# Memory keys and values in float32 inside the experts' ring, expert rows fetched by plain loads and added on VectorE, one more ring tile

## The chip, the cores and the metric

The kernel runs on one core of one Trainium2 chip. The metric is the time of one execution on the device, in microseconds (us); of several runs the median is given.

## What is computed

Two transformer blocks, one after the other, on 512 tokens of width 1024. The first ends in a mixture of 32 experts of which each token uses two; the second mixes sparse attention, a convolution and attention over a memory of 256 rows. Cut to what the change touches:

```python
def hierarchical_moe(h, ...):          # end of the first block
    ...                                # two experts for each token, weights sum to the group's gate
    hid = silu(t @ w1[e]) * (t @ w3[e])
    y = sum over e of combine[:, e] * (hid @ w2[e])
x = x + hierarchical_moe(h2, ...)

def hybrid_layer(x, mem, norm_mix, w_in, ..., norm_mem, w_mem_kv, ...):   # the second block
    xn = rms_norm(x, norm_mix)
    proj = xn @ w_in                   # split into q, kv, gates, conv, q_mem, merge
    ...
    kvm = rms_norm(mem, norm_mem) @ w_mem_kv      # 256 x 1024 by 1024 x 1024
    km, vm = split(kvm)
    ...
```

## The kernel before

**Dense products.** A planner (`Dense`) holds a list of items in program order: weight tiles with their matmuls, and calls. `load` issues the transfer of every item whose ring has room, `prepare` makes the items ready, `step` issues one group of matmuls and, where an item has a `free`, gives its room back. Transfers are issued on SP's queue, in order: a transfer that waits for its tile holds all those behind it. Ordinary weight tiles of 1 MB go through ring "w" (`wraw`, two buffers) and are split into a high and a low part (`whi` by ScalarE at L290, `wlo` by VectorE at L291, two buffers each); a product is then three matmuls, high by high, low by high, high by low (L300 to L302).

**Experts.** 16 pairs of experts (L953 to L978), six tiles of 1 MB to a pair, 96 in all. Their float32 tiles are not split. They go through ring "m", which has no buffers of its own: `room_for` (L243) takes the first place with room among eight `mraw` ("p"), three more ("q"), one `uraw` ("u") and the buffers `wraw`, `whi`, `wlo` ("w", "h", "l", two each), 18 tiles together; `grant` (L178) gives and takes rooms. A pair has its tokens gathered, four tiles of up-projection (L891), then two of down-projection (L907); ScalarE copies the result out (`yt`, L912) and POOL scatters it into the DRAM tensor `y_d` (L913), where each token has two rows.

**Memory.** Midway through the experts, with four rooms taken from "p", `lay_mem` loads the memory, and `lay_mem2` normalises, transposes and splits it into two tiles (`memT`, high and low). After the experts come four column blocks of `w_mem_kv` (L980 to L995): each tile split, 48 matmuls, and a copy to `kvraw` by ScalarE. Blocks 0 and 1 are loaded by SP in ring "m"; blocks 2 and 3 are loaded by POOL's queue, each tied behind another instruction there (`load_behind`, L224).

**From one block to the next.** At L1217 every engine passes a branch for the case in which an expert has more tokens than its 64 places; in these runs it is not taken. Then eight accumulating transfers on POOL's queue add the rows of `y_d` to `x1` (printed as `x` in the trace; L1289 to L1296), four token tiles by two choices. Two column blocks of the second block's `w_in` (columns 2328 and 2584, the memory's queries) are loaded behind them. Per half (two token tiles) ScalarE sums squares (L1310), VectorE makes the reciprocal root and scales (`ny`, L1313), TensorE transposes, ScalarE and VectorE split into `xnT` (L235, L236), and then the `w_in` products begin. `x1` is also stored to DRAM by POOL (L1813).

Of the kernel before, what the change touches and what calls it, by code (L numbers as in the profile page):

```python
# [6 lines left out]
F32 = mybir.dt.float32  # L7
# [5 lines left out]
OP = mybir.AluOpType  # L13
# [8 lines left out]
CAP = 64  # L22
RING = 8
RING2 = 3
NE = 32
US = 1000.0

# [132 lines left out]
def _body(ctx, tc, I, out):  # L160
# [12 lines left out]
    dn = Dense()  # L173
    dn.room["w"] = 2
    dn.room["m"] = 0
    MR = {"room": {"p": 0, "q": 0, "u": 0, "w": 0, "h": 0, "l": 0}}

    def grant(n, at="p"):  # L178

# [38 lines left out]
    def behind(i, j):  # L218

        tc.add_manual_dep(i.ins, j.ins.name,  # L220
                          mybir.DependencyInfo(mybir.DependencyClass.NoSync, mybir.DependencyReason.DATA),
                          reason="order")

    def load_behind(ring, j):  # L224

        MODE["behind"] = j
        dn.room[ring] = 1
        dn.load()
        dn.room[ring] = 0
        MODE.pop("behind")  # L230

    def split_to(hi, lo, src, scale=None):

        if scale is None:
# [7 lines left out]

    def room_for(shape):  # L243

        at = next((a for a in "pquwhl" if MR["room"][a] > 0), "p")
        MR["room"][at] -= 1
        if at in "whl":
            tag = {"w": "wraw", "h": "whi", "l": "wlo"}[at]
            r = wp.tile(shape, F32, name=tag, tag=tag, bufs=2)
        elif at == "u":  # L250
            r = r0.tile(shape, F32, name="uraw", tag="U")
        else:
            r = MR[at].tile(shape, F32, name="mraw", tag="mraw")
        MR[id(r)] = at
        return r
# [12 lines left out]
    def wtile(parts, shape, pieces=None, pool_=(), ring="w"):  # L268

        shape = list(shape)  # L270

        def load():
            r = wp.tile(shape, F32, name="wraw", tag="wraw", bufs=2) if ring == "w" else room_for(shape)
            for dst, src in parts:
                if "behind" in MODE:
                    behind(pool.dma_start(dst(r), src), MODE["behind"])
                else:
                    sync.dma_start(dst(r), src)
            return r

        def split(r):
            if ring == "m":
                MR["room"][MR.pop(id(r))] += 1
            h = wp.tile(shape, F32R, name="whi", tag="whi", bufs=2)
            l = wp.tile(shape, F32R, name="wlo", tag="wlo", bufs=2)
            np_, by_pool = (pieces, pool_) if pieces else MODE["split"]
            n = shape[1] // np_
            for i in range(np_):
                sl = slice(i * n, i * n + n)
                act.activation(h[:, sl], r[:, sl], AF.Copy)  # L290
                (pool if i in by_pool else dve).tensor_tensor(l[:, sl], r[:, sl], raw(h[:, sl]), op=OP.subtract)  # L291
            return h, l
        return load, split
# [603 lines left out]
    def push_down(e):  # L897
        p, m = divmod(e, 2)
        own = slice(64 * m, 64 * m + 64)

        def g(wt):

            hs = HS[p]
            py = psd()
            for k in range(2):
                for q in range(2):
                    pe.matmul(py[64 * q:64 * q + 64], hs[:, k, own], wt[:, k, 512 * q:512 * q + 512],  # L907
                              start=k == 0, stop=k == 1)

            def late():  # L910
                yt = R["ep"].tile([128, 512], F32, name="yt", tag="yt", bufs=4)
                act.activation(yt, py, AF.Copy)  # L912
                st = pool.indirect_dma_start(  # L913
                    out=y_d.rearrange("r (q d) -> (r q) d", q=2),
                    out_offset=bass.IndirectOffsetOnAxis(ap=R["dest2"][:, e:e + 1].bitcast(U32), axis=0),
                    in_=yt, in_offset=None, bounds_check=4 * S - 1, oob_is_err=False)
                for o in ysc:
                    tc.declare_no_dep(st.ins, o, reason="each row belongs to one token and choice")
                ysc.append(st.ins)
                if e == NE - 3:  # L920
                    load_behind("z", st)
            dn.defer(late)
            return 4 * 4 * 216.0
        load, same, free = down_tile(e)
        dn.push(load, same, [g], ring="m", free=free)
# [10 lines left out]

    def lay_mem2():
        raws, gy = memT["x"]
        hl = [MR["p"].tile([128, 8, 256], F32R, name=f"memT{i}", tag="mraw") for i in range(2)]
        for t in range(2):  # L940
            ss, rr = small("nss", [128, 1], 4), small("nrr", [128, 1], 4)
            act.activation(gy[:, 1], raws[:, t], AF.Square, accum_out=ss)
            rsqrt(rr, ss, [128, 1], 1.0 / D, EPS)
            dve.scalar_tensor_tensor(raws[:, t], raws[:, t], rr, gy[:, 0], op0=OP.mult, op1=OP.mult)
            ts_ = slice(t * 128, t * 128 + 128)
            for hf in range(2):
                ps = transpose4(lambda k: raws[:, t, (4 * hf + k) * 128:(4 * hf + k) * 128 + 128])
                ks = slice(4 * hf, 4 * hf + 4)
                split_to(hl[0][:, ks, ts_], hl[1][:, ks, ts_], ps.rearrange("p (k s) -> p k s", k=4))
        memT["T"] = hl  # L950
        grant(2)

    for p in range(NP):  # L953
        push_up(p, 0)
# [9 lines left out]
        else:  # L964
            dn.call(lambda p=p: (dn.flush(), lay_h(p)))
        if p == NP // 2 - 2:
            dn.call(lambda: grant(-4))
        if p == NP // 2:
            dn.call(lay_mem)
        if p == NP - 4:  # L970
            dn.call(lambda: (grant(-2, "h"), grant(-2, "l")))
        if p == NP - 3:
            dn.call(lambda: grant(-1, "u"))
        if p == NP // 2 + 2:
            dn.call(lay_mem2)
    dn.call(lambda: turn_h(NP - 1))
    push_down(NE - 2)
    push_down(NE - 1)  # L978

    dn.call(dn.flush, "experts")  # L980
    for c in range(4):
        def g(wt, c=c):
            if c == 0:
                R["kv"] = r0.tile([128, 2, 2, 512], F32, name="kvraw", tag="U")
            ps = psd()
            for t in range(2):
                ts_ = slice(t * 128, t * 128 + 128)
                for k in range(8):
                    mm3(ps[:, 256 * t:256 * t + 256], memT["T"][0][:, k, ts_], memT["T"][1][:, k, ts_],
                        wt[0][:, k], wt[1][:, k], k == 0, k == 7)  # L990
            a, h = divmod(c, 2)
            dn.defer(lambda: act.activation(R["kv"][:, a, :, h * 256:h * 256 + 256],
                                            ps.rearrange("p (t w) -> p t w", t=2), AF.Copy))
            return 48 * 109.0
        dn.push(*wcols(w_mem, c * 256, 256, ring="m"), [g], ring="m" if c < 2 else "z", name="mem" if c == 3 else None)  # L995

    dn.until("up_b")
    m2s.close()
# [63 lines left out]
    grant(RING - 6)  # L1062
    dn.until("wo3")
    mts.close()
    xes, q2s, es = ExitStack(), ExitStack(), ExitStack()
    xep = sub(xes, "rows", side="right")
    R["xe"] = [xep.tile([128, D], F32, name=f"xe{i}") for i in range(2)]
    MR["q"] = sub(q2s, "moeraw2", RING2, "right")
# [8 lines left out]
    with ordered(nc.vector.engine, nc.scalar.engine, nc.tensor.engine):  # L1077
# [110 lines left out]
            last = dve.tensor_reduce(cw[own], t5[own, :, m], axis=AX.X, op=OP.add)  # L1188
        rts.close()
        R["ep"] = sub(es, "experts", 1, "right")  # L1190
        lay_x(0)

    with tc.issue_after(last.ins):
# [15 lines left out]
    dn.until("experts")  # L1209
    dn.ahead = 1  # L1210
    es.close()
    q2s.close()
    xes.close()

# [2 lines left out]
    with tc.If(nr > 0):  # L1217
        with tc.tile_pool(name="rest", bufs=1, side="right") as fp:
# [57 lines left out]
                        in_=yt, in_offset=None, bounds_check=2 * S - 1, oob_is_err=False)  # L1276


    w_in2 = I["w_in_2"][0]
    w_mo, w_no, w_co, w_o2 = (I[n][0] for n in ("w_mem_out_2", "w_nsa_out_2", "w_conv_out_2", "w_out_2"))  # L1280
    w_g2, w_u2, w_d2 = (I[n][0] for n in ("w_gate_2", "w_up_2", "w_down_2"))
    cw1, cw2 = I["cmp_w1_2"][0], I["cmp_w2_2"][0]
    x2_d = tc.dram_tile([128, 4, D], F32, name="x2_d")
    macc2_d = tc.dram_tile([128, 8, S], F32, name="macc2_d")
    yv = y_d.rearrange("(k t p) d -> p t k d", k=2, p=128)
    dense_N(w_in2, 2328, 256, lambda: xnT, lambda c, q, ps: ev_qm(c, q, ps),
            between=lambda: (lay_xn(2), lay_xn(3)))
    added = []
    for k in range(2):  # L1289
        for t in range(4):  # L1290
            added.append(pool.dma_start(x1[:, t], yv[:, t, k], accum_op=OP.add))
            if (k, t) == (0, 0):
                load_behind("z", added[-1])
            if (k, t) == (1, 1):
                load_behind("w", added[-1])
                dn.room["w"] = -1  # L1296
    brs = ExitStack()
    br_p = sub(brs, "branch", side="right")

# [7 lines left out]
    for q in range(2):  # L1307
        ss, rr = small("nss", [128, 2], 4), small("nrr", [128, 2], 4)
        for t in range(2):
            act.activation(ny[q][:, t], x1[:, 2 * q + t], AF.Square, accum_out=ss[:, t:t + 1])  # L1310
        rsqrt(rr, ss, [128, 2], 1.0 / D, EPS)
        for t in range(2):
            dve.scalar_tensor_tensor(ny[q][:, t], x1[:, 2 * q + t], rr[:, t:t + 1], R["g2"], op0=OP.mult, op1=OP.mult)  # L1313
# [493 lines left out]

    dn.call(lay_kv_mem)
    dense_N(w_in2, 2584, 256, X, lambda c, q, ps: ev_qm(1, q, ps))
    load_behind("w", added[-1])  # L1810
    dn.room["w"] = 1
    for t in range(4):
        behind(pool.dma_start(x2_d[:, t], x1[:, t]), added[-1])  # L1813
    lay_xn(0)
    lay_xn(1)
    dn.call(lambda: lay_qm(0))
# [226 lines left out]
```

## Time and profile before

| | us |
|---|---|
| median of three runs | 1792.62 (1791.51 to 1793.68) |
| the profiled execution | 1795.56 |
| its span in the trace | 1793.5 |
| TensorE busy (PE) | 1692.7, 94% of the span |
| VectorE, ScalarE, GpSimd busy | 947.6, 662.1, 285.7 |
| experts, first matmul to the last weight tile | 603.75 to 832.62 |
| last weight tile of the experts to the second block's first `w_in` block running without a break | 832.62 to 882.90 |

The busy shares are means over stages with different limits. In the experts' stage the transfer engines (DMA) are busy almost without a break; behind 883 us TensorE is; the 50 us between the two are a chain of small transfers, splits and norms.

### The profile page before, as it was taken

Reading aid. Unit: us, or ns where it says so; the run is one execution under the profiler, and the core shown is the slowest. Engines: PE = TensorE matmul, PEld = TensorE weight load, DVE = VectorE, ACT = ScalarE, POOL = GpSimd, SP = SyncE. Lnnn points to the kernel's source line nnn. Section 1 sums busy time; section 2 is a strip of 40 time slices with the busy share of each in tenths; the row PEclk is TensorE's granted clock in tenths of the full one; section 3 lists DMA queues with packets and bytes.
Section 4 is the critical chain, followed back from the end, with each engine's and each line's share of the span. In section 5 each row is a group of like instructions: output and inputs, shape, how many; then the busy total and the mean of one; then the engine's idle time right before and its main releaser. Section 6 shows DMA issues by size and latency. Waiting matters only on the chain.

```text
span 1793.5 us, 24558 instructions
## 1 busy us (share of the span) xinstructions
PE 1692.7 (94%) x9766; PEld 1373.6 (77%) x9766; DVE 947.6 (53%) x2001; ACT 662.1 (37%) x1128; POOL 285.7 (16%) x276
## 2 busy tenths in 40 slices
PE   7999999999999699887799988799999999999999
PEld 7888888889789455444789876588788988888887
DVE  7642367777753411111578789964467444444221
ACT  4222244454523122122435577566523322222111
POOL 1000000000012222112200178611001111111000
PEclk9999999999999799899899999899999999999999
DMA  6223322122348899998724311121243222222240
GB/s 205 94 71 117 118 84 82 48 83 83 141 141 314 324 411 415 418 416 298 218 94 118 118 48 47 71 94 48 88 142 122 83 94 94 94 94 94 83 141 35
DMA packets 151018, 263.87 MB, mean 147 GB/s; under 512 B 11771, under 2 KB 109766, under 8 KB 146550
## 3 DMA queue, kind: packets, MB, share of 16 engines
q1 hardware_dynamic: 131542, 220.03, 34.2%
q0 software_dynamic: 12400, 33.71, 6.1%
q10 hardware_dynamic: 6960, 8.56, 1.3%
q8 instruction: 77, 1.26, 0.3%
q14 instruction: 39, 0.32, 0.1%
HBM read 248.62 MB, written 18.87 MB: 149 GB/s over the span
## 4 chain that ended last, share of the span: by engine, by line
PE 41%; DVE 7%; ACT 2%; DMA 2%; issue 1%; POOL 0%; ACTq 0%; DVEq 0%; POOLq 0%
PE pd L300 11%; PE pd L301 11%; PE pd L302 11%; DVE oa L1756 3%; PE pa L301 2%; PE pa L300 2%; PE pa L302 2%; DMA x<-y_d 2%; DVE wlo L291 1%; PE pa L381 1%; PE pa L1646 1%; ACT whi L290 1%; DVE sn L1661 0%; DVE sden L1668 0%; DVE pt L236 0%
## 5 line engine op out<-in xcount | busy, mean ns | idle before, releaser
L291 DVE TENSOR_TENSOR wlo<-wraw,whi 128x2048 fp32r<-128x2048 f32 (+1 forms) x112 | 248.8, 2221 | 192.8 <-ACT whi L290 192.1
L290 ACT ACTIVATE whi<-wraw 128x2048 fp32r<-128x2048 f32 (+1 forms) x123 | 213.1, 1735 | 345.8 <-PE pd L301 198.8
L301 PE MATMUL pd<-wlo,hT 128*128 128x256 f32 x512 | 145.5, 284 | 1.5 <-DVE wlo L291 1.5
L300 PE MATMUL pd<-whi,hT 128*128 128x256 f32 x512 | 146.0, 285 | 0.0
L302 PE MATMUL pd<-whi,hT 128*128 128x256 f32 x512 | 145.2, 284 | 0.0
L302 PE MATMUL pd<-hnT,wlo 128*128 128x512 f32 x352 | 139.4, 396 | 0.0
L300 PE MATMUL pd<-hnT,whi 128*128 128x512 f32 x352 | 139.3, 396 | 0.0
L301 PE MATMUL pd<-hnT,whi 128*128 128x512 f32 x352 | 139.2, 395 | 0.0
L300 PE MATMUL pd<-xnT,whi 128*128 128x512 f32 (+1 forms) x280 | 114.3, 408 | 0.0
L301 PE MATMUL pd<-xnT,whi 128*128 128x512 f32 (+1 forms) x280 | 113.0, 404 | 0.0
L302 PE MATMUL pd<-xnT,wlo 128*128 128x512 f32 (+1 forms) x280 | 112.9, 403 | 0.0
L1750 POOL TENSOR_TENSOR oa<-oa,ctm 128x512 f32<-128x512 f32 x60 | 91.3, 1522 | 60.5 <-ACT ctm L1749 57.0
L301 PEld LDWEIGHTS pd<-wlo,hT 128*128 128x128 f32 x512 | 97.2, 190 | 2.6 <-DVE wlo L291 1.8
L300 PEld LDWEIGHTS pd<-whi,hT 128*128 128x128 f32 x512 | 97.4, 190 | 1.2 <-issue 0.9
L302 PEld LDWEIGHTS pd<-whi,hT 128*128 128x128 f32 x512 | 97.1, 190 | 0.9 <-issue 0.4
L870 DVE SCALAR_TENSOR_TENSOR sg<-sg,pd 128x256 f32<-128x256 f32 x16 | 6.7, 421 | 165.6 <-ACT sg L869 165.6
L891 PE MATMUL pd<-mraw,xs 128*64 128x256 f32 x624 | 77.6, 401 | 11.8 <-DMA mraw<-in_w 11.6
L300 PEld LDWEIGHTS pd<-hnT,whi 128*128 128x128 f32 x352 | 66.1, 188 | 16.0
L301 PEld LDWEIGHTS pd<-hnT,whi 128*128 128x128 f32 x352 | 66.1, 188 | 15.9
L302 PEld LDWEIGHTS pd<-hnT,wlo 128*128 128x128 f32 x352 | 66.1, 188 | 15.8
L300 PE MATMUL pd<-hT,whi 128*128 128x512 f32 x192 | 77.8, 405 | 0.0
L302 PE MATMUL pd<-hT,wlo 128*128 128x512 f32 x192 | 77.7, 405 | 0.0
(546 smaller groups left out, 4059.1 us busy)
## 6 DMA issues: line engine op xcount, KB each, us to landing
mraw<-in_w SPq DMA_DIRECT2D x59, 1024.0 KB
wraw<-in_w_in SPq DMA_DIRECT2D x41, 1024.0 KB
wraw<-in_w_gate SPq DMA_DIRECT2D x19, 1024.0 KB
wraw<-in_w SPq DMA_DIRECT2D x11, 1024.0 KB
wraw<-in_w_up SPq DMA_DIRECT2D x11, 1024.0 KB
wlo<-in_w SPq DMA_DIRECT2D x10, 1024.0 KB
whi<-in_w SPq DMA_DIRECT2D x10, 1024.0 KB
wraw<-in_w_down SPq DMA_DIRECT2D x10, 1024.0 KB
```

The lines of the kernel that those rows point to most:

```text
L290: act.activation(h[:, sl], r[:, sl], AF.Copy)
L291: (pool if i in by_pool else dve).tensor_tensor(l[:, sl], r[:, sl], raw(h[:, sl]), op=OP.subtract)
L300: pe.matmul(ps, ah, bh, start=start, stop=False)
L301: pe.matmul(ps, ah, bl, start=False, stop=False)
L302: pe.matmul(ps, al, bh, start=False, stop=stop)
L381: pe.transpose(ps[:, t * 128:t * 128 + 128], src_of(t), ident)
L870: dve.scalar_tensor_tensor(sg, sg, 1.0, hid[:, 0:256], op0=OP.add, op1=OP.mult)
L891: pe.matmul(ph[64 * m:64 * m + 64, 256 * j:256 * j + 256], XS[p][:, kt, 64 * m:64 * m + 64], wt[:, m, k], start=kt == 0, stop=kt == 7)
L1646: pe.matmul(ps[:, :nm], Q[:, 4 * g + i, qs], KS[:, br, g, x, :nm], start=x == 0, stop=x == 1)
L1750: pool.tensor_add(acc, acc, tm)
L1756: taps.append(lambda i=i: dve.scalar_tensor_tensor(acc, up[:, j, i:i + S], convw[:, i, j:j + 1], acc, op0=OP.mult, op1=OP.add))
```

## The change

The memory is kept as one float32 tile: no split, and each column block takes 16 float32 matmuls in place of 48. The tiles of `w_mem_kv` become items of the experts' ring as the experts' own are (`whole`): block 0 stands between two pairs of experts, blocks 1 to 3 directly behind the last expert. The rows of `y_d` are fetched by four plain loads of 1 MB on SP's queue into tiles `yk` of the ring, and eight additions on VectorE put them on `x1`; the accumulating transfers and `load_behind` go. A new place "s" holds one more ring tile, in memory that the router leaves free; "u" is taken away five pairs earlier and the two "w" rooms two pairs before the end; three rooms instead of four are taken for the memory. The `w_in` block 2328 becomes an item ahead of the point at which the planner stands when the experts end.

```diff
@@ room_for
-        at = next((a for a in "pquwhl" if MR["room"][a] > 0), "p")
+        at = next((a for a in "pqsuwhl" if MR["room"][a] > 0), "p")
@@ lay_mem2
-        hl = [MR["p"].tile([128, 8, 256], F32R, name=f"memT{i}", tag="mraw") for i in range(2)]
+        mT_ = MR["p"].tile([128, 8, 256], F32, name="memT", tag="mraw")
...
-                split_to(hl[0][:, ks, ts_], hl[1][:, ks, ts_], ps.rearrange("p (k s) -> p k s", k=4))
-        memT["T"] = hl
+                act.activation(mT_[:, ks, ts_], ps.rearrange("p (k s) -> p k s", k=4), AF.Copy)
+        memT["T"] = mT_
         grant(2)
+
+    def push_mem(c):
+        def g(wt):
+            if c == 0:
+                R["kv"] = r0.tile([128, 2, 2, 512], F32, name="kvraw", tag="U")
+            ps = psd()
+            for t in range(2):
+                ts_ = slice(t * 128, t * 128 + 128)
+                for k in range(8):
+                    pe.matmul(ps[:, 256 * t:256 * t + 256], memT["T"][:, k, ts_], wt[:, k], start=k == 0, stop=k == 7)
+            a, h = divmod(c, 2)
+            dn.defer(lambda: act.activation(R["kv"][:, a, :, h * 256:h * 256 + 256],
+                                            ps.rearrange("p (t w) -> p t w", t=2), AF.Copy))
+            return 64 * 109.0
+        v = w_mem.rearrange("(k p) c -> p k c", p=128)
+        load, same, free = whole(v[:, :, c * 256:c * 256 + 256], (128, 8, 256))
+        dn.push(load, same, [g], ring="m", free=free, name="mem" if c == 3 else None)
@@ experts' loop
-            dn.call(lambda: grant(-4))
+            dn.call(lambda: grant(-3))
         if p == NP // 2:
-            dn.call(lay_mem)
+            dn.call(lambda: (lay_mem(), grant(-1, "u")))
         if p == NP - 4:
             dn.call(lambda: (grant(-2, "h"), grant(-2, "l")))
         if p == NP - 3:
-            dn.call(lambda: grant(-1, "u"))
+            push_mem(0)
+        if p == NP - 2:
+            dn.call(lambda: grant(-2, "w"))
...
     push_down(NE - 2)
+    dn.call(lambda: dn.room.update(w=2))
     push_down(NE - 1)
 
     dn.call(dn.flush, "experts")
...
+    for c in range(1, 4):
+        push_mem(c)
+    w_in2 = I["w_in_2"][0]
+    dense_N(w_in2, 2328, 256, lambda: xnT, lambda c, q, ps: ev_qm(c, q, ps),
+            between=lambda: (lay_xn(2), lay_xn(3)))
@@ router's end
         rts.close()
         R["ep"] = sub(es, "experts", 1, "right")
+        MR["s"] = sub(q3s, "moeraw3", RING3)
+        grant(RING3, "s")
+        dn.load()
         lay_x(0)
@@ behind the branch
-    for k in range(2):
-        for t in range(4):
-            added.append(pool.dma_start(x1[:, t], yv[:, t, k], accum_op=OP.add))
...
+    yk = {}
+    for t in range(4):
+        yk[t] = MR["p"].tile([128, 2, D], F32, name="yk", tag="mraw")
+        sync.dma_start(yk[t], yv[:, t])
...
         for t in range(2):
+            for k in range(2):
+                dve.tensor_add(x1[:, 2 * q + t], x1[:, 2 * q + t], yk[2 * q + t][:, k])
             act.activation(ny[q][:, t], x1[:, 2 * q + t], AF.Square, accum_out=ss[:, t:t + 1])
```

The planner and the scheduler turn this into an order of instructions. On SP before, the second round of the experts' ring, 18 tiles, has its two `wraw` side by side (`in_w` are the experts' weights):

```order
L261 DMA mraw<-in_w 128x2x1024
L261 DMA uraw<-in_w 128x2x1024
L261 DMA wraw<-in_w 128x2x1024 x2
L261 DMA whi<-in_w 128x2048 x2
L261 DMA wlo<-in_w 128x2x1024 x2
```

After, on SP in the same round, the two turns of `wraw` are apart:

```order
L254 DMA uraw<-in_w 128x2x1024
L254 DMA wraw<-in_w 128x2048
L254 DMA whi<-in_w 128x2x1024 x2
L254 DMA wraw<-in_w 128x2048
L254 DMA wlo<-in_w 128x2x1024 x2
```

They are apart because a `w_in` tile (`in_w_in`, block 2328) has one of the two buffers; after, it stands on SP between the first expert tiles of the ring, while the products of `w_out` run:

```order
L268 DMA wraw<-in_w_up_b 128x8x256
L268 DMA wraw<-in_w_out 128x8x256 x4
L254 DMA mraw<-in_w 128x2x1024 x4
L268 DMA wraw<-in_w_in 128x8x256
L254 DMA mraw<-in_w 128x2x1024 x4
```

It keeps the buffer until it is split, towards the end of the experts, so that the ring has one `wraw` left of the two that were granted, and the second load of each round waits until TensorE is through with the first: 18 tiles in effect, as before.

On SP before, the end of the experts is two blocks of the memory and the branch:

```order
L261 DMA mraw<-in_w 128x2048 x2
L261 DMA wraw<-in_w 128x2048
L261 DMA mraw<-in_w 128x2048
L278 DMA mraw<-in_w_mem_kv 128x8x256 x2
L1217 COMPARE_AND_BRANCH
```

After, on SP, blocks 1 to 3 of the memory stand there, then two `w_in` tiles ahead of the branch:

```order
L254 DMA mraw<-in_w 128x2048 x4
L254 DMA mraw<-in_w_mem_kv 128x8x256 x2
L254 DMA wraw<-in_w_mem_kv 128x8x256
L1218 TENSOR_LOAD rounds
L1218 ISA x2
L268 DMA wraw<-in_w_in 128x8x256 x2
L1219 COMPARE_AND_BRANCH
```

and on SP behind the branch come the four loads of the expert rows:

```order
L1235 COMPARE_AND_BRANCH
L1235 UNCONDITIONAL_BRANCH
L1219 UNCONDITIONAL_BRANCH
L1290 DMA yk<-y_d 128x2x1024 x4
L268 DMA wraw<-in_w_in 128x8x24
```

Each of the two `w_in` loads ahead of the branch waits until VectorE has split the tile before it (2328, then 2584); the four `yk` loads now stand behind that.

On VectorE before, behind the branch, there are the splits of the memory's last blocks and the first half's norm:

```order
L1217 UNCONDITIONAL_BRANCH
L291 TENSOR_TENSOR wlo<-mraw,whi 128x2048 x3
L353 TENSOR_SCALAR rs_v<-nss 128x2
L354 TENSOR_SCALAR rs_i<-rs_v 128x2
L355 TENSOR_SCALAR nrr<-rs_i 128x2
```

After, the additions stand there, all eight of them ahead of the first half's `ny`:

```order
L1219 UNCONDITIONAL_BRANCH
L1305 TENSOR_TENSOR x_4749<-x_4749,yk 128x1024 x5
L343 TENSOR_SCALAR rs_v<-nss 128x2
L1305 TENSOR_TENSOR x_4749<-x_4749,yk 128x1024
L344 TENSOR_SCALAR rs_i<-rs_v 128x2
L345 TENSOR_SCALAR nrr<-rs_i 128x2
L348 TENSOR_TENSOR rs_a<-nrr 128x2
L349 SCALAR_TENSOR_TENSOR rs_a<-rs_a,rs_v 128x2
L350 SCALAR_TENSOR_TENSOR nrr<-rs_a,nrr 128x2
L1305 TENSOR_TENSOR x_4749<-x_4749,yk 128x1024
L351 TENSOR_TENSOR rs_a<-nrr 128x2
```

The additions of the second half have moved ahead of the first half's scaling.

## Rows read from the trace of the kernel before

**Rows 1.** The page: span, and busy time of each engine.

```profile
span 1793.5 us, 24558 instructions
PE 1692.7 (94%) x9766; PEld 1373.6 (77%) x9766; DVE 947.6 (53%) x2001; ACT 662.1 (37%) x1128; POOL 285.7 (16%) x276
```

**Rows 2.** Windows: stretch, length, busy of five engines, PE clock, DMA share, GB/s.

```profile
604.00:608.00 4.00, 4.00 (x28) 2.33 (x28) 1.05 (x5) 0.00 (x0) 0.99 (x1) 0.70 0.20 55
608.00:612.00 4.00, 4.00 (x40) 2.43 (x36) 0.00 (x0) 0.00 (x0) 0.00 (x0) 1.00 0.94 314
607.00:832.60 225.60, 202.21 (x1424) 109.19 (x1421) 31.65 (x73) 43.82 (x86) 44.03 (x43) 0.97 1.01 408
...
848.00:868.00 20.00, 17.54 (x148) 17.13 (x147) 4.59 (x2) 6.08 (x6) 8.43 (x11) 1.00 1.03 231
...
900.00:1000.00 100.00, 99.46 (x776) 93.14 (x775) 83.32 (x191) 48.84 (x91) 2.36 (x5) 1.00 0.41 125
```

**Rows 3.** Timeline of the experts, PE and SP's queue: start, length, engine, line, idle before.

```profile
603.75 8.41 PE L891 MATMUL pd<-mraw,xs 128*64 128x256 f32 x64
...
607.03 17.50 SPq L261 DMA_DIRECT2D mraw<-in_w  x9
...
700.41 1.95 PE L891 MATMUL pd<-mraw,xs 128*64 128x256 f32 x16
...
720.21 3.68 PE L891 MATMUL pd<-mraw,xs 128*64 128x256 f32 x16 [3.39 <-DMA mraw<-in_w]
725.45 3.68 PE L891 MATMUL pd<-mraw,xs 128*64 128x256 f32 x16 [1.56 <-DMA mraw<-in_w]
...
733.95 1.95 PE L891 MATMUL pd<-mraw,xs 128*64 128x256 f32 x16
```

**Rows 4.** Timeline from the last expert tile on, all engines.

```profile
832.62 1.94 PE L907 MATMUL pd<-mraw,hs 128*64 128x512 f32 x8 [0.64 <-DMA mraw<-in_w]
...
836.25 1.91 ACT L290 ACTIVATE whi<-mraw 128x2048 fp32r<-128x2048 f32 x1 [1.01 <-DMA mraw<-in_w_mem_kv]
838.20 2.29 DVE L291 TENSOR_TENSOR wlo<-mraw,whi 128x2048 fp32r<-128x2048 f32 x1 [12.22 <-ACT whi L290]
...
838.22 0.38 PE L300 MATMUL pd<-whi,memT 128*128 128x256 f32 x1 [3.66 <-ACT whi L290]
...
841.69 1.91 ACT L290 ACTIVATE whi<-mraw 128x2048 fp32r<-128x2048 f32 x1 [3.52 <-DMA mraw<-in_w_mem_kv]
...
844.98 0.41 PE L300 MATMUL pd<-whi,memT 128*128 128x256 f32 x1
...
845.23 0.99 POOL L1291 DMA_DIRECT2D x<-y_d  x1 [8.69 <-DMA y_d<-yt,dest]
...
845.50 0.28 PE L300 MATMUL pd<-whi,memT 128*128 128x256 f32 x1
...
845.62 0.28 PE L301 MATMUL pd<-wlo,memT 128*128 128x256 f32 x1
```

**Rows 5.** The chain of waits, in order of time: start, length, what.

```profile
848.03 15.29 DMA x<-y_d
...
863.84 12.74 DMA x<-y_d
...
882.90 0.58 PE pd L302
```

**Rows 6.** Timeline ahead of the first `w_in` product, all engines.

```profile
876.60 1.06 ACT L1310 ACTIVATE ny<-x 128x1024 f32<-128x1024 f32 x1 [1.39 <-DMA x<-y_d]
...
877.66 0.58 ACT L992 ACTIVATE kvraw<-pd 128x512 f32<-128x512 f32 x1
...
879.77 2.48 DVE L1313 SCALAR_TENSOR_TENSOR ny<-x,nrr,gain 128x1024 f32<-128x1024 f32 x2
```

**Rows 7.** Timeline of PE, a float32 product of the first block (L705).

```profile
260.59 0.39 PE L705 MATMUL pa<-vb,aT 128*128 128x128 f32 x2
...
263.40 0.61 PE L705 MATMUL pa<-vb,aT 128*128 128x128 f32 x4
```

More of the change, by code (lines that the diff above doesn't have):

```diff
@@ L24 @@
 RING2 = 3
+RING3 = 1
 NE = 32
@@ L175, in _body @@
     dn.room["m"] = 0
-    MR = {"room": {"p": 0, "q": 0, "u": 0, "w": 0, "h": 0, "l": 0}}
+    MR = {"room": {"p": 0, "q": 0, "s": 0, "u": 0, "w": 0, "h": 0, "l": 0}}
     def grant(n, at="p"):
@@ L222, in behind @@
                           reason="order")
[L224 to L230, printed above, removed]
     def split_to(hi, lo, src, scale=None):
@@ L274, in load @@
             for dst, src in parts:
[L275 to L278, printed above, removed]
+                sync.dma_start(dst(r), src)
             return r
@@ L919, in late @@
                 ysc.append(st.ins)
-                if e == NE - 3:
-                    load_behind("z", st)
             dn.defer(late)
@@ L977, in _body @@
     push_down(NE - 2)
+    dn.call(lambda: dn.room.update(w=2))
     push_down(NE - 1)
     dn.call(dn.flush, "experts")
[L981 to L995, printed above, removed]
+    for c in range(1, 4):
[3 more added lines that the diff above has]
+            between=lambda: (lay_xn(2), lay_xn(3)))
     dn.until("up_b")
@@ L1064, in _body @@
     mts.close()
-    xes, q2s, es = ExitStack(), ExitStack(), ExitStack()
+    xes, q2s, es, q3s = ExitStack(), ExitStack(), ExitStack(), ExitStack()
     xep = sub(xes, "rows", side="right")
@@ L1211, in _body @@
     es.close()
+    q3s.close()
     q2s.close()
@@ L1276, in _body @@
                         in_=yt, in_offset=None, bounds_check=2 * S - 1, oob_is_err=False)
-    w_in2 = I["w_in_2"][0]
     w_mo, w_no, w_co, w_o2 = (I[n][0] for n in ("w_mem_out_2", "w_nsa_out_2", "w_conv_out_2", "w_out_2"))
@@ L1285, in _body @@
     yv = y_d.rearrange("(k t p) d -> p t k d", k=2, p=128)
-    dense_N(w_in2, 2328, 256, lambda: xnT, lambda c, q, ps: ev_qm(c, q, ps),
-            between=lambda: (lay_xn(2), lay_xn(3)))
-    added = []
-    for k in range(2):
-        for t in range(4):
-            added.append(pool.dma_start(x1[:, t], yv[:, t, k], accum_op=OP.add))
[L1292 to L1296, printed above, removed]
+    yk = {}
+    for t in range(4):
+        yk[t] = MR["p"].tile([128, 2, D], F32, name="yk", tag="mraw")
+        sync.dma_start(yk[t], yv[:, t])
     brs = ExitStack()
@@ L1809, in _body @@
     dense_N(w_in2, 2584, 256, X, lambda c, q, ps: ev_qm(1, q, ps))
-    load_behind("w", added[-1])
-    dn.room["w"] = 1
     for t in range(4):
-        behind(pool.dma_start(x2_d[:, t], x1[:, t]), added[-1])
+        pool.dma_start(x2_d[:, t], x1[:, t])
     lay_xn(0)
```

## The prediction

> **What bounds the kernel now.** I read the page first, then the windows, then the timelines at both ends of the experts and the chain of waits between. TensorE is busy for 94% of the span [rows 1], and behind 900 us it has no gap left, 99.46 of 100 us [rows 2]. What the change touches can therefore win only where TensorE waits: in the experts and in the passage to the second block. In the experts the transfers are the limit. TensorE begins at 603.75 at two tiles in 4 us and lives on the 18 tiles that are already there; SP's first load into a freed place goes out at 607.03, and from 720.21 on TensorE waits for tiles, 3.39 and 1.56 us at a time [rows 3]. From 607 to 832.6 the transfer engines are full, share 1.01 at 408 GB/s [rows 2]. I call the release of the last tile E; before, E = 832.62 [rows 4]. Behind E the chain is one of transfers: the first memory block lands, is split on ScalarE (1.91 us) and VectorE (2.29 us), the accumulating transfers start at 845.23, as soon as the last scatter of expert rows has landed [rows 4], and two of them stand in the chain with 15.29 and 12.74 us [rows 5], at 231 GB/s with the engines full [rows 2]. The `w_in` products run without a break from 882.90 [rows 5], E + 50.3.
>
> **The end of the experts.** All sums are against the profiled execution, 1795.56 us, which lies 2.9 above the median of 1792.62; I carry the difference over to the median. Since the transfers are full until E, each transfer that moves ahead of E costs its own time. Block 0 of `w_mem_kv` does. An expert tile takes 1.05 MB / 408 GB/s = 2.6 us at the stage's rate [rows 2]; the memory blocks have shorter rows, and three of them landed between 832.62 and 841.69 [rows 4], 3.0 us each. I take **+3.1**, nearer the second. Block 2328 of `w_in` moves ahead to the `w_out` stage, where the ring's last loads before 607 leave the transfer engines at a share of 0.20 [rows 2]: nothing. But it keeps a `wraw` until it is split, so that the new tile "s" only makes up for it (18 places in effect, as before), and the second `wraw` load of a ring round waits for TensorE to finish the tile of the first. SP is in order; all loads behind wait as well. The queue must then hold enough to keep the transfer engines busy. Five such loads come: for tiles 14, 33, 52, 68 and 84 of 96. At the first, TensorE is done with the tile before at about 631.7 (14 tiles of 2.0 us), while ten loads were issued since 607.03, 10 x 2.6 = 26 us, so the engines are dry at about 633 to 634: two us of cover. At the next two I get about 670 against 672.5, and 716 to 719 against 718; at the last two TensorE runs just behind the transfers and the loads ahead were issued long before. So 0 to 2 us are lost, **+1.0** taken. E comes 4.1 us later.
>
> **The passage.** Steps are counted from the new E. Blocks 1, 2, 3 and the `w_in` block 2584 are in one queue, 3.0 us each: they land at +3.0, 6.1, 9.1 and 12.1. A float32 product leaves two records for a matmul; L705 has 0.39 us for two and 0.61 for four [rows 7], 0.11 each for 128 columns. A memory block is 16 matmuls of 256 columns, so 16 x 2 x 2 x 0.11 = 7.0 us; 48 split matmuls took 0.12 each at full clock (845.50 to 845.62 [rows 4]), 5.6 us. Block 1 thus runs to +10, block 2 to +17, block 3 to +24. That costs nothing as long as it ends before the expert rows are on `x1`. The splits of the memory's blocks, 4 x (1.9 + 2.3) us, are gone, and with them the first wait of TensorE behind E: 3.66 us and then half clock, 0.41 us a record against 0.28 [rows 4]. The copy of block 1 to `kvraw` (0.58 us [rows 6]) stands on ScalarE ahead of the split of 2584: +10.7. That split goes +12.2 to +14.1 on ScalarE and to +16.5 on VectorE; SP waits for it with its next `w_in` load, then takes the branch, and issues the `yk` loads at about **+17.8**. The scatters' rows are there long before: 845.23 is E + 12.6. So the wait is not the data but SP's order.
>
> The next `w_in` block is ahead in the queue, 3 us; each `yk` is 1 MB in rows of 4 KB, as the experts' tiles have them, 2.6 us: they are there at about +24.8, 27.3, 29.8 and 32.4. The trace has no such load of `y_d`. Below, the bound is 4 x 2.6 from the issue on, +28.2 for the last; above, the same bytes at the 231 GB/s of the accumulating transfers, 4 x 4.5 + 3, +38.8. I take 2.6, since a load reads a row once where accumulation reads and writes the destination as well. An addition on 1024 columns is bounded by half the 2048-column subtraction, 1.15 us, and by `ny`, 1.24 each; the eight hide behind the loads but for the last two. The first half's `ny` stands behind all eight: last load +32.4, two additions to +34.8, the rest of the reciprocal root 0.6, `ny` 2.5 [rows 6], transposes, copies and differences some 3. The `w_in` products then run from about **+41.2**, where they ran from E + 50.3: **−9.1**.
>
> Two things behind it move: `kmv` and `sq` come ahead of the second half's copies on ScalarE, and that half's root goes in between the differences on VectorE. I put **+0.9** for it, with 0 and 2 as bounds (ScalarE's 0.6 us copies, three of them). POOL loses eight transfers and four loads; its stores of `x1` go out behind the additions, earlier than before, and `kmv`, which waits for them, is within the same bounds. The sum is 3.1 + 1.0 − 9.1 + 0.9 = **−4.1**: 1791.5 in the profiled execution, **1788.5** on the median's scale.
>
> **The rivals.** *The ring runs dry* (slower). The cover at tiles 14, 33 and 52 is two us or less by my count, made from mean rates. Gathers for a pair and the uneven pace at 720 shift it by more. What a dry queue costs is to be seen at 607.03: the first load goes out there with the engines at a share of 0.20, and within 608 to 612 they are at 0.94 [rows 2, 3], so that each dry wait costs its length and about 1.5 us of start. If three waits come 3 us too late, 3 x 4.5 = 13.5 in place of 1.0: 1788.5 + 12.5 = **1801**; two of 3 us give 1796.5. It decides the sign once the experts lose more than 5 us to it. The Trainium skill ("DMA: Bandwidth & Descriptors", the section on the anatomy of one DMA) says that a wait is made on the issuing sequencer before dispatch, and that a transfer has a fixed part of about 2 us; by that, five dry waits alone would be 10 us, an estimate, and the time about 1797.5. The rows at 607 agree that a dry queue takes a microsecond or two to come back.
>
> *Half clock in the memory blocks* (no change). After a wait of 3.39 us at 720.21 a tile took 3.68 us, twice its 1.95 [rows 3]. Behind E TensorE waits for block 1 about 1.1 us (end of the last tile at +1.94, landing at +3.0); after 1.56 us at 725.45 the tile was slow too, but had been slow before [rows 3]. At half clock block 1 takes 14 us and its copy comes 7 us later; the split of 2584 behind it then starts at +17.8 in place of +12.2, and the `yk` loads 5 to 5.6 us later: 1788.5 + 5.3 = **1794**. The Trainium skill ("TensorE: Matmul & The Clock Gate", on what is actually happening) puts it that throttled is the default and activity releases it; the same rows show that, and if each short wait of the experts' end counted, this case would be the likelier one.
>
> *SP is early* (faster). If the transfers of `y_d` go out before the splits are done, or the experts do not end later, because fewer `wraw` loads wait than I think and the clock holds through the ring, then the 5 us of cost fall to 1 or the `yk` loads come 4 us earlier, each for itself: **1784**, and both **1780**.
>
> **How the numbers follow.** Changes under 0.2%, 3.6 us, can't be told from none here. I give my sum 0.50; its own error, mostly from the loads' rate and the 0 to 2 us of the waits, is about 3 us, so that 0.34 of it is faster, 0.15 same, 0.01 slower. The dry ring has 0.20 (0.17 slower, 0.03 same), half clock 0.15 (0.11 same, 0.04 slower), early SP 0.15, all faster. Faster 0.49, same 0.29, slower 0.22. The range goes from early SP's 1780 to 1799, past two dry waits of 3 us, and leaves three of them, or `yk` loads at the accumulating rate on top of half clock, outside.
>
> **What would show it.** The last expert tile's release should be at about 836.7 if all before stays in place; at 840 or more, the ring ran dry, and the windows from 630 to 720 will show shares under 1. TensorE's wait behind it should be near 1 us and the memory blocks 7 us each; 14 means half clock. The `yk` loads should be issued 18 us behind E and land at 2.6 us one from the other; the additions should wait for them and nothing else. The `w_in` products should run from about E + 41. It would all be wrong if TensorE lost its full cover behind 900.

## The result and the profile after

The changed kernel takes 1803.29 us (median of seven runs, 1800.75 to 1809.70) beside 1792.14 us for the kernel before: 1.0066 times as long, 95% interval 1.0053 to 1.0079, **slower by some 11 us** where 4 us less were forecast, and outside the range. The profiled execution has a span of 1804.7 us.

Three marks divide the stretch that the change touches: S, the first product of the experts; E, the release of the last expert tile; and M, the transposes of the first normalised queries and the memory's keys, which all kernels here have alike and behind which all take 885 to 887 us to the end. From the traces:

| us | S | E | M | S to E | E to M |
|---|---|---|---|---|---|
| before | 603.75 | 832.62 | 908.23 | 228.9 | 75.6 |
| after | 600.98 | 852.47 | 918.61 | 251.5 | 66.1 |

The passage behind the experts is 9.5 us shorter, and the experts are 22.6 us longer. (S lies 2.8 us earlier after; the last section has why that is not the change's.)

The windows of after, in stretches of 20 us and four of 4 us; after the length come the busy times of PE, PEld, DVE, ACT and POOL, then PE clock, DMA share, GB/s:

```profile
620.00:640.00 20.00, 19.41 (x144) 10.67 (x142) 1.60 (x3) 4.23 (x8) 5.09 (x5) 1.00 0.98 374
660.00:680.00 20.00, 17.37 (x122) 9.86 (x120) 2.19 (x4) 3.84 (x8) 5.08 (x5) 0.91 0.82 312
700.00:720.00 20.00, 14.25 (x98) 7.81 (x96) 2.29 (x4) 3.52 (x7) 4.25 (x5) 0.92 0.96 382
760.00:780.00 20.00, 14.31 (x95) 7.47 (x92) 1.22 (x3) 2.32 (x5) 3.30 (x4) 0.91 0.64 229
820.00:840.00 20.00, 15.92 (x120) 9.19 (x118) 3.10 (x3) 4.24 (x6) 2.59 (x2) 1.00 0.86 323
664.00:668.00 4.00, 4.00 (x36) 2.68 (x32) 0.42 (x1) 0.74 (x2) 0.00 (x0) 1.00 0.20 78
752.00:756.00 4.00, 2.84 (x12) 1.90 (x14) 3.72 (x11) 0.00 (x0) 1.99 (x1) 0.50 1.04 431
760.00:764.00 4.00, 3.31 (x29) 2.06 (x26) 0.00 (x0) 0.66 (x2) 0.27 (x1) 1.00 0.27 108
764.00:768.00 4.00, 4.00 (x34) 2.33 (x32) 0.69 (x1) 0.00 (x0) 1.04 (x1) 1.00 0.16 22
```

Before, the same stage ran at a share of 1.01 and 408 GB/s [rows 2]. Against the 416 GB/s of a full window the five long ones lose 2.0, 5.0, 1.6, 9.0 and 4.5 us of transfer; the window from 800 to 820, in which the last of the waits begins, loses another 1.7 (380 GB/s). From 760 to 768 the transfer engines stand nearly still, in the stage that they bound. SP's queue at the beginning of the experts and there, start, length, issue:

```profile
599.45 18.08 SPq L254 DMA_DIRECT2D mraw<-in_w  x9
...
742.74 6.15 SPq L254 DMA_DIRECT2D whi<-in_w  x2
767.55 0.38 SPq L254 DMA_DIRECT2D wraw<-in_w  x1
767.98 0.46 SPq L254 DMA_DIRECT2D wlo<-in_w  x1
768.49 22.33 SPq L254 DMA_DIRECT2D mraw<-in_w  x11
```

Nothing goes out from 749 to 767.55; then the second `wraw` of the round does, and the loads behind it follow from 767.98 on. TensorE ran the tile that this load waited for just ahead of it (765.56, the round's first `wraw`), behind a wait of 3.36 us for the memory's norm and a stretch at half clock (0.50 granted from 752 to 756), and then waits for what was issued too late:

```profile
753.16 1.97 PE L371 MATMUL pa<-ident,memn 128*128 128x128 f32 x8 [3.36 <-DVE memn L932]
...
765.56 1.95 PE L881 MATMUL pd<-wraw,xs 128*64 128x256 f32 x16
...
775.58 3.29 PE L881 MATMUL pd<-wraw,xs 128*64 128x256 f32 x16 [4.64 <-DMA wraw<-in_w]
```

The waits of SP at the second turn, 640 to 668 (what it waited for: sum, times, longest):

```profile
SPq L254 <- PE pd L881: 19.5, 2, 18.0
```

It stood 18.0 us before one load, from 649 to 667; the transfers queued ahead of it lasted to about 664.5, so that the share from 664 to 668 is 0.20.

Behind E, the timeline of after answers to [rows 4] and [rows 6]:

```profile
852.47 1.94 PE L897 MATMUL pd<-mraw,hs 128*64 128x512 f32 x8 [0.49 <-DMA mraw<-in_w]
855.72 14.05 PE L949 MATMUL pd<-mraw,memT 128*128 128x256 f32 x64 [1.31 <-DMA mraw<-in_w_mem_kv]
862.90 0.60 ACT L951 ACTIVATE kvraw<-pd 128x512 f32<-128x512 f32 x1 [7.81 <-PE pd L949]
864.61 1.91 ACT L280 ACTIVATE whi<-wraw 128x2048 fp32r<-128x2048 f32 x1 [1.11 <-DMA wraw<-in_w_in]
...
870.32 1.92 SPq L1290 DMA_DIRECT2D yk<-y_d  x4
877.05 6.35 DVE L1305 TENSOR_TENSOR x<-x,yk 128x1024 f32<-128x1024 f32 x5 [8.20 <-DMA yk<-y_d]
...
888.81 2.48 DVE L1309 SCALAR_TENSOR_TENSOR ny<-x,nrr,gain 128x1024 f32<-128x1024 f32 x2 [0.35 <-DMA x_d<-x]
...
890.20 3.22 PE L371 MATMUL pa<-ident,ny 128*128 128x128 f32 x14 [13.13 <-issue]
```

The two memory blocks take 7.0 us each at full clock behind a wait of 1.31 us, the split of 2584 holds SP, the `yk` loads go out at E + 17.85, the first addition starts at E + 24.6, and the products follow the transposes without a break from 893.84, E + 41.4.

### The profile page after: what moved, and what is told of

It reads as the page before. It is cut to its first block, busy times and chain, and to the rows that moved or that the text cites. A ratio compares the mean times of both kernels' runs of the same rounds, so it can differ in the third digit from the quotient of the medians.

```text
span 1804.7 us, 24368 instructions
## 1 busy us (share of the span) xinstructions
PE 1696.5 (94%) x9702; PEld 1373.8 (76%) x9702; DVE 945.0 (52%) x2001; ACT 655.9 (36%) x1124; POOL 274.2 (15%) x264
## 4 chain that ended last, share of the span: by engine, by line
PE 42%; DVE 6%; ACT 2%; issue 1%; DMA 1%; SPq 0%; ACTq 0%; DVEq 0%
PE pd L290 11%; PE pd L291 11%; PE pd L292 11%; DVE oa L1752 2%; PE pa L291 2%; PE pa L290 2%; PE pa L292 2%; PE pa L371 2%; DVE wlo L281 1%; PE pa L1642 1%; DMA yk<-y_d 1%; ACT whi L280 1%; PE pa L1623 1%; PE pa L1624 0%; DVE sden L1664 0%
## 5 line engine op out<-in xcount | busy, mean ns | idle before, releaser
L281 DVE TENSOR_TENSOR wlo<-wraw,whi 128x2048 fp32r<-128x2048 f32 (+1 forms) x112 | 247.6, 2210 | 233.2 <-ACT whi L280 211.8
L290 PEld LDWEIGHTS pd<-hnT,whi 128*128 128x128 f32 x352 | 66.1, 188 | 16.0
L291 PEld LDWEIGHTS pd<-hnT,whi 128*128 128x128 f32 x352 | 66.1, 188 | 15.9
L292 PEld LDWEIGHTS pd<-hnT,wlo 128*128 128x128 f32 x352 | 66.1, 188 | 15.8
L290 PE MATMUL pd<-hT,whi 128*128 128x512 f32 x192 | 77.5, 403 | 0.0
L291 PE MATMUL pd<-hT,whi 128*128 128x512 f32 x192 | 76.9, 400 | 0.0
```

Source lines behind the costliest of these rows:

```text
L290: pe.matmul(ps, ah, bh, start=start, stop=False)
L291: pe.matmul(ps, ah, bl, start=False, stop=False)
L292: pe.matmul(ps, al, bh, start=False, stop=stop)
```

## The experiments

**Theory A**: the experts' ring was granted two `wraw` while block 2328 held one of them; SP, being in order, waits at each second turn for TensorE's previous tile, with every later load behind it, and the transfer engines run dry. **Rival B**: the memory's blocks in the ring, with their short rows, and the rooms that move lengthen the experts. **Rival C**: the plain loads gain nothing, the passage was long for the memory's splits. All of the next rows are medians and intervals against the kernel before on the same chip, and the stretches of one trace each:

| run | median us | ratio (95%) | S to E | E to M |
|---|---|---|---|---|
| e1 one wraw place | 1783.18 | 0.9938 (0.9921 to 0.9954) | 231.7 | 62.4 |
| e2 2328 late | 1784.49 | 0.9946 (0.9929 to 0.9963) | 228.6 | 68.4 |
| e3 2328 late, accumulating | 1795.97 | 1.0015 (1.0005 to 1.0024) | 229.2 | 77.7 |
| e4 2328 late, yk first | 1782.39 | 0.9935 (0.9918 to 0.9952) | 229.0 | 64.3 |
| e5 second place from pair 9 on | 1784.34 | 0.9958 (0.9945 to 0.9971) | 233.2 | 61.8 |
| e6 before, ring tile alone | 1784.53 | 0.9954 (0.9938 to 0.9971) | 227.0 | 69.8 |
| e7 before, float32 memory alone | 1791.09 | 0.9995 (0.9985 to 1.0004) | 228.7 | 73.0 |
| e8 as e4, block 0 behind the experts | 1786.52 | 0.9968 (0.9956 to 0.9981) | 227.0 | 71.3 |
| e9 second place until pair 9 | 1795.89 | 1.0016 (1.0007 to 1.0026) | 243.3 | 63.2 |
| e10 before, u granted twice | 1803.88 | 1.0055 (1.0038 to 1.0072) | 246.0 | 69.3 |

**One place less (e1).** The ring stays at 18 places in effect, since the second was never free:

```diff
-    grant(2, "w")
+    grant(1, "w")
...
-            dn.call(lambda: grant(-2, "w"))
+            dn.call(lambda: grant(-1, "w"))
```

> The changed kernel with one wraw place granted to the experts' ring in place of two (and one taken back): the ring no longer counts on the buffer that the early w_in tile 2328 holds, and no load on SP waits for the tile just ahead of it. Places in effect stay 18. Theory A (the loads that wait for that buffer dry SP's queue): experts from first matmul to last tile 251.5 us before this edit, now 232 to 236, and about 1786 us; the yk loads also come out ahead of the w_in loads in SP's order, which may take off 3 us more. Rival B (the float32 memory block in the ring, its short rows and the rooms that move are what costs): experts stay over 245 us, 1798 to 1803.

The experts fall from 251.5 to 231.7 us and the kernel to 1783.18, 20 us under the changed one and 9 to 11 under the kernel before. Windows of this run, as above:

```profile
660.00:680.00 20.00, 20.00 (x150) 10.88 (x148) 2.01 (x4) 4.22 (x8) 5.82 (x6) 1.00 1.03 414
760.00:780.00 20.00, 15.69 (x108) 7.34 (x103) 2.50 (x5) 4.97 (x10) 3.03 (x3) 1.00 1.02 416
```

The dry windows are gone with the granted place; block 0 of the memory, the short rows and the moved rooms are all still there. Rival B falls. The `yk` loads stand ahead of the `w_in` loads in this order, and the passage is 3.7 us shorter than after's.

**Block 2328 late (e2).**

```diff
     for c in range(1, 4):
         push_mem(c)
-    w_in2 = I["w_in_2"][0]
-    dense_N(w_in2, 2328, 256, ...)
...
         sync.dma_start(yk[t], yv[:, t])
+    w_in2 = I["w_in_2"][0]
+    dense_N(w_in2, 2328, 256, ...)
```

> The changed kernel with the w_in block 2328 pushed behind the yk loads in the program, as the kernel before has it: both wraw buffers are free for the ring, 19 places in effect, and 1 MB more is loaded behind the experts. Theory A: experts 231 to 235 us, no dry window from 620 to 820; passage (last tile to w_in products running) 41 as after, since the two w_in loads still stand ahead of the branch but wait for no split: 38 to 42; 1782 to 1787 us. Rival B: experts over 245 us, 1798 to 1803.

The other way to free the buffer gives the same: 228.6 us of experts, 3.1 less than e1 with one place more, and 1784.49. The passage is 2.3 us longer than after's, against a forecast of 38 to 42 for the products: they run from E + 43, since the splits of 2328 now lie there as well.

**The expert rows (e3, e4).** e3 puts the accumulating transfers back into e2:

```diff
-    yk = {}
     for t in range(4):
-        yk[t] = MR["p"].tile([128, 2, D], F32, name="yk", tag="mraw")
-        sync.dma_start(yk[t], yv[:, t])
+        for k in range(2):   # k outside, t inside, as before
+            pool.dma_start(x1[:, t], yv[:, t, k], accum_op=OP.add)
...
-                dve.tensor_add(x1[:, 2 * q + t], x1[:, 2 * q + t], yk[2 * q + t][:, k])
```

> As the run with 2328 late, but the expert rows added to x1 by the eight accumulating transfers on POOL's queue as before, no yk loads and no additions on VectorE. Theory A with my passage: the accumulating transfers cost what they did, 28 us on the chain from E + 12.6 on, so 6 to 9 us slower than the run with yk, about 1792. Rival C (the plain loads gain nothing, the passage was long because of the memory blocks' splits and their POOL loads): within 2 us of the run with yk.

The passage is 77.7 us in place of 68.4 and the median 11.5 us higher. TensorE's wait ahead of the first normalised rows, in e2 and then in e3:

```profile
869.69 3.65 PE L371 MATMUL pa<-ident,ny 128*128 128x128 f32 x16 [14.28 <-issue]
```

```profile
880.04 3.60 PE L371 MATMUL pa<-ident,ny 128*128 128x128 f32 x16 [24.52 <-issue]
```

Rival C falls: seen from E, the rows are there 10.0 us sooner with the plain loads and additions, and the median moves by more than the 6 to 9 us expected. e4 ties the two `w_in` loads of e2 behind the last `yk` load (an order alone, no wait):

```diff
             for dst, src in parts:
-                sync.dma_start(dst(r), src)
+                i = sync.dma_start(dst(r), src)
+                if MODE.get("after"):
+                    behind(i, MODE["after"].pop())
...
+    MODE["after"] = [yd, yd]   # yd: the last yk load
```

> As the run with 2328 late, with the two w_in loads tied behind the last yk load. If the yk loads wait for SP's order, they go out at E + 13 (last scatter landed) or when the memory blocks are through the queue, and the w_in products start 3 to 6 us earlier than with the w_in loads ahead: 1778 to 1783. If they wait for the scatters or the chain is on VectorE anyway: within 1 us of that run; if the w_in blocks are then late for their split, slower by up to 3.

The `yk` loads go out at 840.45, E + 10.5, as the last scatter lands, and not at E + 18.6; the passage is 64.3 us, 4.1 shorter. This is the lowest median of the study, 1782.39 us, 0.9935 of the kernel before; e1's 1783.18 can't be told apart from it.

**The memory alone, and its place (e7, e8).** e7 has the kernel before with `push_mem` for all four blocks directly behind the experts, and nothing else of the change:

```diff
-        hl = [MR["p"].tile([128, 8, 256], F32R, ...) for i in range(2)]
+        mT_ = MR["p"].tile([128, 8, 256], F32, name="memT", tag="mraw")
...
     dn.call(dn.flush, "experts")
     for c in range(4):
-        ...                    # split, 48 matmuls
+        push_mem(c)
```

> The kernel before with the memory part alone: keys and values in float32, the four blocks as unsplit ring items directly behind the experts, expert rows by accumulating transfers as before, no extra tile. If the splits of the memory's blocks were off the path that the accumulating transfers set: 1791 to 1795, with TensorE's wait behind the last tile down from 3.66 to about 1.1 us and full clock in the blocks. If the accumulating transfers were late because they shared the engines with the blocks' POOL loads: up to 5 us faster, 1787.

1791.09 us, no change: the accumulating transfers set the end as before, the first square on ScalarE waits 15.47 us for them. TensorE's wait behind the last tile is 1.85 us in place of 3.66, the blocks run at full clock, and in the median that neither costs nor wins anything: the one trace has a passage 2.6 us shorter, the medians are 0.6 us apart, and the interval contains 1. e8 moves block 0 of e4 behind the experts:

```diff
         if p == NP - 3:
-            push_mem(0)
+            pass
...
-    for c in range(1, 4):
+    for c in range(4):
         push_mem(c)
```

> The run with yk first, with block 0 of the memory behind the experts instead of inside the ring. The experts should be 3.0 us shorter (one short-row tile less). Behind them TensorE has four blocks of 7 us in place of three, up to E + 31, and the copy of the last block stands ahead of the squares on ScalarE: products from E + 43 to 45 in place of E + 38, so 1784 to 1787, 2 to 4 us slower than the run with yk first. If the squares don't wait for the last block: 1779 to 1781.

The experts are 2.0 us shorter, not 3.0, and the passage 7.0 longer, one block's time: its copy stands on ScalarE ahead of the squares. Block 0 is well placed inside the ring.

**The ring tile alone (e6).**

```diff
-        at = next((a for a in "pquwhl" if MR["room"][a] > 0), "p")
+        at = next((a for a in "pqsuwhl" if MR["room"][a] > 0), "p")
...
+        MR["s"] = sub(q3s, "moeraw3", RING3)
+        grant(RING3, "s")
+        dn.load()
```

> The kernel before with the one more ring tile alone (19 places, none of them blocked). The tile is loaded in the stretch before 607 in which the transfer engines are nearly idle, so one tile less is left for the saturated stretch: experts 226 in place of 228.9 us and 1789 to 1791 if a tile's transfer is what it gains; nothing, 1792 to 1794, if the experts' length is set by something other than the transfers.

The experts are 227.0 us, 1.9 less, about what a tile loaded in the idle stretch should give. But the median is 1784.53, 7 us under before, and the passage 5.8 us shorter, which neither hypothesis had. Part of it lies ahead of the first half's `ny`, which starts at E + 37.7 in place of E + 40.0. For the rest, VectorE has another order behind that `ny`. Before, the second half's `ny` starts at 879.77 [rows 6], and the first half's differences follow it at 882.16:

```profile
872.58 2.48 DVE L1313 SCALAR_TENSOR_TENSOR ny<-x,nrr,gain 128x1024 f32<-128x1024 f32 x2 [0.42 <-DMA x<-y_d]
...
882.16 3.08 DVE L236 TENSOR_TENSOR xnT<-pa,xnT 128x512 fp32r<-128x512 f32 x5
```

In this run the first half's four differences come first:

```profile
871.60 2.48 DVE L1318 SCALAR_TENSOR_TENSOR ny<-x,nrr,gain 128x1024 f32<-128x1024 f32 x2 [0.42 <-DVE nrr L365]
...
877.40 0.69 DVE L237 TENSOR_TENSOR xnT<-pa,xnT 128x512 fp32r<-128x512 f32 x1
...
879.42 0.68 DVE L237 TENSOR_TENSOR xnT<-pa,xnT 128x512 fp32r<-128x512 f32 x1
880.67 2.29 DVE L292 TENSOR_TENSOR wlo<-wraw,whi 128x2048 fp32r<-128x2048 f32 x1
883.07 2.48 DVE L1318 SCALAR_TENSOR_TENSOR ny<-x,nrr,gain 128x1024 f32<-128x1024 f32 x2
```

The first half's products then run while the second half is normalised. An edit elsewhere made the scheduler choose another order; e10, below, has the same order, `ny` at E + 37.0 and a passage of 69.3 us. So with the same accumulating transfers the kernel before loses some 6 us of passage against both; 2 to 3 of them lie ahead of `ny`, and about 3.5 are left for the order on VectorE. No run changes that order alone, so its price is not shown, nor how the 7 us divide between tile and order.

**Which of the waits (e5, e9).** Here the second place is granted late (e5), or taken back early (e9):

```diff
-            dn.call(lambda: (lay_mem(), grant(-1, "u")))
+            dn.call(lambda: (lay_mem(), grant(-1, "u"), grant(1, "w")))    # e5, from e1
+            dn.call(lambda: (lay_mem(), grant(-1, "u"), grant(-1, "w")))   # e9, from after
```

> The run with one wraw place, with the second place granted at the ninth pair: the first three waits of the changed kernel (tiles 14, 33, 52) are absent, two or three in the second half of the experts come back. By my prediction's step the late waits cost nothing, since TensorE runs just behind the transfers: as with one place, 1782 to 1785. By the windows of the changed kernel (760 to 780 at a share of 0.64, 816 to 824 at 0.69 and 0.31) they are the dear ones: experts 10 to 14 us longer than with one place, 1793 to 1797, and dry windows behind 740 alone.

> The changed kernel with the second wraw place taken back at the ninth pair: the turns at tiles 14, 33 and 52 remain as they are, those at 68 and 84 have one place. By the shares of the changed kernel's windows the first three cost 2.0, 5.0 and 1.6 us and the last two 9.0 and 4 to 5: experts 237 to 240 us in place of 251.5, and 1789 to 1793. By the step of my prediction, in which the last two cost nothing: experts 250, 1800 to 1803.

Neither isolated the two late waits. In e5 the granted place has two turns on SP:

```profile
748.10 0.37 SPq L254 DMA_DIRECT2D wraw<-in_w  x1
...
789.43 1.83 SPq L254 DMA_DIRECT2D wraw<-in_w  x1
```

The first comes four tiles behind the tile whose buffer it needs. SP stands 14.0 us before it, most of which the transfers in flight cover; its window is the one mild one, 3.3 us of transfer lost:

```profile
740.00:760.00 20.00, 17.39 (x117) 9.18 (x117) 1.62 (x4) 3.01 (x6) 3.03 (x3) 0.92 0.90 347
```

The second comes six tiles behind; SP waits 1.7 us for TensorE there, and the transfer engines stay full. The experts are 1.5 us longer than in e1. The 1784.34 us lie in the range expected of late waits that cost nothing, but these are not the changed kernel's late turns, so nothing follows for those. A place without a buffer is nearly free where the transfers in flight cover the wait for its turn.

In e9 the fourth turn was still there, 3.0 us sooner than in after, and only the last one went. SP's load there, and the window around it:

```profile
764.52 0.38 SPq L254 DMA_DIRECT2D wraw<-in_w  x1
```

```profile
760.00:780.00 20.00, 14.75 (x86) 7.10 (x85) 1.60 (x3) 1.85 (x4) 3.02 (x3) 0.83 0.81 301
```

Experts of 243.3 us, 11.6 over e1, answer to four waits. The 8.2 us under after are not the fifth's alone: the fourth's window lost 5.5 us here in place of 9.0, with a wait for the memory's norm of 1.12 us on TensorE in place of 3.36. Both hypotheses' figures, 237 to 240 and 250, miss: the late waits are not free, but what each costs alone is not shown.

**The cause by itself (e10).** The kernel before, where nothing of the change stands, with the one-buffer place "u" granted twice:

```diff
-    grant(1, "u")
+    grant(2, "u")
...
-            dn.call(lambda: grant(-1, "u"))
+            dn.call(lambda: grant(-2, "u"))
```

> The kernel before with the place u granted twice, which has one buffer: nothing else changes, and no place more is there in effect, but in each round the second load for it waits until TensorE is through with the tile of the first, with SP's queue behind it. If that alone is the cause: dry windows between 620 and 830, experts 240 to 252 us in place of 228.9, 1802 to 1815. If it is the w_in tile, the float32 memory block or the moved rooms that the changed kernel suffers from: 1790 to 1794.

The experts take 246.0 us, 17.1 more, and the kernel 1803.88. That this is almost the changed kernel's 1803.29 is chance: there the experts are 5.5 us longer and the passage 3.1 shorter. What counts is the stage, which loses here by this one edit nearly what it lost there. Its dry windows, and one of TensorE's waits for the second tile:

```profile
660.00:680.00 20.00, 20.00 (x158) 12.24 (x155) 1.60 (x3) 3.63 (x7) 4.98 (x5) 1.00 0.83 310
740.00:760.00 20.00, 14.23 (x66) 6.72 (x62) 6.12 (x24) 3.64 (x7) 0.99 (x1) 0.67 0.80 330
760.00:780.00 20.00, 14.13 (x90) 7.66 (x90) 1.60 (x3) 2.27 (x4) 2.53 (x3) 0.83 0.77 294
```

```profile
819.95 3.68 PE L891 MATMUL pd<-uraw,xs 128*64 128x256 f32 x16 [7.76 <-DMA uraw<-in_w]
```

Theory A holds, in both directions: the place taken away from after gives 19.8 us of the experts back (20 of the median), a false place given to before costs 17.1 (12 of the median, with a passage 6.3 us shorter).

## Why the prediction was wrong

- **The waits of the ring: wrong, and alone enough.** The step that failed is the term for SP's waits, "So 0 to 2 us are lost, +1.0 taken": between after and e1, which differ in that place, lie 19.8 us of experts. Two parts of it failed. At tiles 14, 33 and 52 I set mean rates against each other, got a cover of two us or less, and took the cover for enough; the windows lost 2.0, 5.0 and 1.6 us. At tile 33 the term for TensorE was right, done at S + 66.0 (forecast S + 66.3), and that for the queue was not: its transfers ended at about S + 63.5, not S + 68.8. The forecast counted them from 607.03, S + 3.3 in the kernel before; after, the ring's loads begin with the new tile at 599.45, S − 1.5, and the same 65.5 us (672.5 − 607.03) from there end at 664.9, about where they did end. A cover within the error of its two terms was a coin's toss, to be priced at a few us each. And "at the last two TensorE runs just behind the transfers and the loads ahead were issued long before" was wrong in kind: at tile 68 TensorE had just stood 3.36 us for the memory's norm and was at half clock in parts, and SP's wait for it outlasted the queue, 9.0 us of transfer; in e9, with a shorter wait for the norm, 5.5. The delay was then paid by both, SP until 767.55 and TensorE with 4.64 us at 775.58.
- **The mechanism stood among the rivals.** The dry ring had 1801 us for three late waits of 3 us; 1803.29 was measured. What was wrong was its chance of 0.20, and a range that ended at 1799. That the figure came so near is luck in part: it priced the waits at 13.5 us, where 19.8 were measured, and S was 2.8 us sooner in the trace of after. The Trainium skill's rule ("DMA: Bandwidth & Descriptors", the anatomy of one DMA) that a wait is made on the issuing sequencer agrees with SP's 18.0 us before one load. The estimate by its fixed part of a transfer, 1797.5, came nearer than my sum, but for another reason: the loss was the length of the waits, not the restart; and that section of the Trainium skill gives the fixed part for transfers issued by GpSimd, where these are SP's.
- **Block 0 in the ring: right.** +3.1 forecast; e1 against before 2.8 with the same 18 places, e8 against e4 2.0. (Of the three landings that it was read from, [rows 4] shows two.)
- **The new tile "s" only makes up for the one held: right** in effect (e1 has 18 places); worth 3.1 us once both `wraw` are free (e2 against e1).
- **The passage: right.** `yk` issued at E + 17.85 (forecast 17.8), first addition at E + 24.6 (24.8), products from E + 41.4 (41.2), blocks of 7.0 us at full clock (7.0). With what follows the passage to M is 9.5 us shorter; 9.1 less 0.9 was forecast. That SP's order and not the data holds the loads is shown by e4: 8 us sooner, seen from E. What the plain loads are worth depends on the order beside them: 9.3 us between e3 and e2, but e6 and e10, with accumulating transfers and another order on VectorE, come within 3.7 us of after's 66.1. My account of the passage compared after with before's order and was right for that pair alone.
- **Half clock in the memory blocks: did not come,** the wait ahead of them was 1.31 us. **Nor was SP early,** by the E + 17.85 above.

With the wait term at 19.8 in place of 1.0, the sum would have been 14.7 us above before; 11 were measured, and S, which differs by 2.8 us between the two traces, covers most of the rest.

## What to carry to other kernels

A ring that borrows buffers must be granted no more places than it can have at its worst moment. Where an in-order queue issues the loads, one place without a buffer can cost not that place but all loads behind it: read the order for two turns of the same buffer, and price each by the wait of the queue less what is in flight, with a spread as wide as the errors of both. A gain in a passage of 50 us can be exact to half a microsecond and lost in a stage that the change seemed only to graze: count what an item that is moved up holds while it waits.

## What was unexpected

S differs by up to 6 us between traces of kernels that are the same up to there: 600.48 to 606.83. It goes with the clock that TensorE was granted in the first block's attention. The windows from 300 to 400 us of before, of after, of e1 and of e6, in this order:

```profile
300.00:400.00 100.00, 98.22 (x599) 82.21 (x597) 69.24 (x214) 47.81 (x103) 9.25 (x11) 0.95 0.24 70
```

```profile
300.00:400.00 100.00, 98.27 (x618) 82.72 (x618) 71.47 (x224) 48.84 (x105) 9.28 (x11) 0.98 0.25 74
```

```profile
300.00:400.00 100.00, 97.98 (x597) 82.11 (x597) 69.60 (x214) 47.93 (x102) 9.26 (x11) 0.95 0.23 67
```

```profile
300.00:400.00 100.00, 97.79 (x589) 81.40 (x589) 69.96 (x212) 49.02 (x100) 9.21 (x11) 0.95 0.22 64
```

Granted 0.95, S was 603.75, 604.53 and 606.83; granted 0.98, 600.98, with fewer products done in the same time in the first case. The other eight traces have 0.97 to 1.00 there, and S at 600.48 to 602.56. So a profile's absolute times are good to some 6 us here, and stretches were compared from a mark within each trace. What decides the clock there was not tried.
